# First feed-forward of a hybrid layer: table batches in finer steps, three sums in each, and four queues held to the text's order

## Chip, cores and metric

The kernel runs on one core of one Trainium2 chip. The metric is the device time of one execution in microseconds (us), the median of several runs. Engines are named as the profile names them: PE (TensorE, the matrix engine; PEld is its weight load), DVE (VectorE), ACT (ScalarE), POOL (GpSimd) and SP (SyncE, whose queue issues most DMAs here; "SPq" in the rows).

## The reference, cut to what matters

One decoder layer for 1024 tokens of width 1024, all in f32:

```python
mod = silu(cond) @ w_mod + b_mod              # nine vectors of 1024
h = modulate(rms_norm(x, ffn1_norm), sh1, sc1)
x = x + 0.5 * g1 * swiglu(h, w_gate, w_up, w_down)          # first feed-forward, d_ff = 2816
h = modulate(rms_norm(x, mix_norm), sh2, sc2)
b, c, v, u = split(h @ w_in)
y_conv = b * conv3_causal(c * v)
y_ssm  = GLU(Re(C . state) + D * u)           # 32 groups, 64 complex states each
x = x + g2 * ([rms_norm(y_conv) | rms_norm(y_ssm)] @ w_out)
x = x + 0.5 * g3 * swiglu(modulate(rms_norm(x, ffn2_norm), sh3, sc3), ...)   # second feed-forward
return rms_norm(x, final_norm)
```

Two kinds of side work do not depend on the tokens, and the kernel does them during the first feed-forward: the **modulation sums** (rows of `w_mod` times the activated condition, one row block of 128 x 1024 after another) and the **tables of the state space model** (powers of its eigenvalues times B and C), which the mixing stage reads later.

## The kernel before, in words

Every f32 product is three matrix products of rounded parts: each operand is a high part (fp32r) and a low part, and `mm3` issues high x high, high x low, low x high, 128 x 512 each. A weight tile `w` gets its parts in `Weights.pump`: ACT casts the raw tile to the high part, DVE subtracts to get the low part; the raw tile came by a DMA on SP, and some raw tiles get a second block added by a DMA on POOL.

The first feed-forward has 11 groups of 256 hidden channels, `fa0` to `fa10`. Groups 1 to 10 run in `seven`: gate and up projections as seven block products each (left operands A11, S1, S2, S4, S3, A12, A22, in that order for groups 2 to 10). One of the seven is 24 matrix products of 128 x 512, gate side then up side. They gather in three PSUM banks a side, called B, C and A; a bank is read out (ACT copies it to `t1`, `c1` or `u2`, or DVE adds it to one of these) before the next product in that bank may start. The products of a finished group go to DRAM (`kept1` to `kept10`). Then `down7`, twice (`fad0`, `fad1`), does the down projection of groups 1 to 8, again as seven products; it needs the kept blocks back as left operands: `fetch` loads one from DRAM on SP, ACT casts it, DVE subtracts (`fa1lA11` is block A11 of group 1). The fetches for `fad0` are issued inside `fa10`, four after each of its products. Groups 0, 9 and 10 follow in `last_parts` (tiles `fald`).

The side work is a Python generator, `side1`. A `Clock` counts the `mm3` calls; after every `period` ticks it runs the generator to its next `yield`, so the instructions of that step stand at that place in the program's text. The period is `BATCH_PERIOD` during the tables. The tables are made in eight batches, `ssm_batch(0)` to `ssm_batch(7)`. One batch: load `prm`; DVE makes `bb`, then `cl` (with a second term `clt`), `bl` (with `blt`) and the rotors `rot`, `rott`, from a pool of four buffers tagged `bt`; PE multiplies `bl` and `cl` into `kp` and transposes `bl` into `tp`, 8 short instructions; ACT copies these to `kc` and `mi` (again `bt` buffers); DVE corrects `kc`; SP stores all to DRAM: `mo_d` from `cl`, `co_d` and `si_d` from the rotors, `mk_d` from `kc`, `mi_d` from `mi`. `gate1` is one modulation sum: `mod_tile` lets DVE do the sum over the oldest loaded tile (`ISA wm...` in the program order) and SP load the next one; there are two such tiles.

Before group 10 starts, the text says (lines 1355 to 1361)

```python
if g == NGRP - 1:
    while clock.side:
        clock.step()
    side_open.close()
    ...
    open_x(ctx)
    load_x(range(2), (0, 2))
```

so whatever is left of the batches is written down at once between `fa9` and `fa10`; the memory of the tables is then given back, and four loads of `x` go into it.

The order in which an engine gets its instructions is not always the text's. A scheduler lays the program out ahead of time from its own idea of when things are ready, engine by engine, and may move an instruction past others of the same engine. `InOrder` wraps VectorE, ScalarE, TensorE and SyncE: while `InOrder.strict` is true, each instruction issued through it is tied behind the one before on that engine, so that this engine keeps the text's order. GpSimd is not wrapped. Before the change, strict order holds in the prologue alone. At run time every engine takes its instructions strictly one after the other.

Of the kernel before, what the change touches and what calls it, by code (L numbers as in the profile page):

```python
# [13 lines left out]
F32 = mybir.dt.float32  # L14
# [214 lines left out]
def hymba_layer(ctx: ExitStack, tc, x_d, xt_d, wm1_d, wmod_d, gu1_d, gs1_d, ds1_d, wl1_d, win_d, wout_d, glu_d, gu2_d, gs2_d, wd2_d, ds2_d, wl2_d, cols_d, cond_d, lam_d, bc_d, out_d):  # L229
# [771 lines left out]

    cact_d = scratch.tile([P, 1024], F32, name="cact_d")
    SP.dma_start(cact_d[:], cact[:])
    mk_d = scratch.tile([NB, P, GB * P], F32, name="mk_d")
    mi_d = scratch.tile([NB, P, GB * P], F32, name="mi_d")
    mo_d = scratch.tile([NB, P, GB * P], F32, name="mo_d")
    co_d = scratch.tile([NB, P, GB * P], F32, name="co_d")
# [25 lines left out]
    def ssm_base(sb, sb1):  # L1033
# [127 lines left out]
            yield  # L1161
        zero = sb1.tile([CH, 112], F32, name="zero")
        V.memset(zero[:], 0.0)
        mk4 = mk_d[:].rearrange("b p (g c) -> p b g c", g=GB)
        for t in range(1, TAU):
            for b in range(NB):
                SP.dma_start(
                    mk4[t * CH : (t + 1) * CH, b, :, 0 : t * CH],
                    zero[:, 0 : t * CH].unsqueeze(1).to_broadcast([CH, GB, t * CH]),
                )  # L1170
            yield
        ssm.update(q=qq, tabs=tabs, base=baset, step=step, lam=lam)

    def ssm_batch(b):
        bp = bps[0]
        gs = slice(b * GB, (b + 1) * GB)
        prm = bp.tile([P, 4, GB, CH], F32, tag="prm", name=f"prm{b}")
        SP.dma_start(prm[:], bc_d[b])
        bb = bp.tile([P, 2, GB, CH], F32, tag="bb", name=f"bb{b}")
        q = tuple(ssm["q"][:, i, gs].unsqueeze(2).to_broadcast([P, GB, CH]) for i in range(2))  # L1180
        cmul(bp, bb[:], prm[:, 0:2], q, [GB, CH], f"bb{b}")
        p1, p2, e1, e2 = ssm["tabs"]

        def bt(name):
# [12 lines left out]
        cl = bt(f"cl{b}")
        cl4 = cl[:].rearrange("p (g n c) -> p g n c", g=GB, n=9)
        yield from comb(cl4, 9, (p1, p2), (prm[:, 2], prm[:, 3]), ALU.add, f"clt{b}")
        SP.dma_start(mo_d[b].rearrange("p (g m) -> p g m", g=GB), cl4[:, :, 1:9, :].rearrange("p g n c -> p g (n c)"))  # L1200
        bl = bt(f"bl{b}")
        bl4 = bl[:, :512].rearrange("p (g n c) -> p g n c", g=GB, n=8)
        yield from comb(bl4, 8, (e1, e2), (bb[:, 0], bb[:, 1]), ALU.add, f"blt{b}")
        if b >= 2:
            yield from gate1()

        def v3(a):
            return a[:, :512].rearrange("p (g m i) -> p g m i", g=GB, m=8)

        bs = [a[:, gs, :].unsqueeze(2).to_broadcast([P, GB, 8, 16]) for a in ssm["base"]]  # L1210
        st = [ssm["step"][:, i, :, gs].rearrange("p m g -> p g m").unsqueeze(3).to_broadcast([P, GB, 8, 16]) for i in range(2)]

        def rotors():

            r, t = bt(f"rot{b}"), bt(f"rott{b}")
            V.tensor_tensor(out=v3(r), in0=st[0], in1=bs[0], op=ALU.mult)
            V.tensor_tensor(out=v3(t), in0=st[1], in1=bs[1], op=ALU.mult)
            yield
            V.tensor_tensor(out=r[:, :512], in0=r[:, :512], in1=t[:, :512], op=ALU.add)
            A.activation(t[64:128, :512], r[64:128, :512], AF.Copy, scale=-1.0)  # L1220
            for half in (slice(0, 64), slice(64, 128)):
                SP.dma_start(co_d[b, half], r[0:64, :512])
            SP.dma_start(si_d[b, 0:64], r[64:128, :512])
            SP.dma_start(si_d[b, 64:128], t[64:128, :512])

        yield from rotors()
# [10 lines left out]
        if b >= 2:  # L1237
            yield from gate1()
            yield from gate1()
            yield from gate1()  # L1240
        kc = bt(f"kc{b}")
        kc3 = kc[:CH, :512].rearrange("p (g m) -> p g m", g=GB)
        A.copy(kc[:CH, :512], kp[:])
        for g in range(GB):
            V.scalar_tensor_tensor(
                out=kc3[:, g, 0:CH], in0=ident[:CH, :CH], scalar=ssm["lam"][:CH, 3, b * GB + g : b * GB + g + 1], in1=kc3[:, g, 0:CH], op0=ALU.mult, op1=ALU.add
            )
        mk3 = mk_d[b].rearrange("p (g m) -> p g m", g=GB)
        for t in range(TAU):
            SP.dma_start(mk3[t * CH : (t + 1) * CH, :, t * CH :], kc3[:, :, : P - t * CH])  # L1250
        mi = bt(f"mi{b}")
        A.copy(mi[:, :512], tp[:])
# [39 lines left out]
    def side1():  # L1292
        yield from combos1()
        clock.period = 4.5
        sb = side_open.enter_context(tc.tile_pool(name="sb", bufs=1, side="right"))
        with tc.tile_pool(name="sb1", bufs=1, side="right") as sb1:
            yield from ssm_base(sb, sb1)
        clock.period = BATCH_PERIOD
        bps.append(side_open.enter_context(tc.tile_pool(name="bp", bufs=1, side="right")))
        mod_home.pool = side_open.enter_context(tc.tile_pool(name="wmp", bufs=1, side="right"))  # L1300
        share[0] = MODS[1]
        for _ in range(2):
            mod_fetch(mod_home)
        for b in range(NB):
            yield from ssm_batch(b)

    def side2(home, n):

# [16 lines left out]
            norm_into(act2, h, n2[h], 1, "h2")  # L1325

    movs["B"] = es1.enter_context(tc.tile_pool(name="movB1", bufs=12))
    BATCH_PERIOD = 5.5
    first_open = ExitStack()

    def first_opened():
# [32 lines left out]
        seven(f"fa{g}", kept=kept[g], order=SOON if g == 1 else SEVEN, then=(lambda left: fetch_chunk(0, left)) if g == NGRP - 1 else None)  # L1364
    down7("fad0", lefts[0], 0, lambda left: fetch_chunk(1, left), lambda left: load_x(range(2), (1, 3)) if left == "A12" else None)
    down7("fad1", lefts[1], 0, fetch_last)
    clock.period = 4
    clock.side.append(side2(mod_mov, MODS[2]))
    pools["mixed"] = False
# [454 lines left out]
```

## Time and profile before

| what | value |
|---|---|
| time, median of 3 runs | 1688.69 us (1688.16 to 1690.33) |
| profiled execution, its own time | 1691.52 us |
| its span, first to last instruction | 1689.7 us |
| instructions | 20647 |
| PE busy | 1657.2 us, 98% |
| DVE, ACT, POOL busy | 63%, 40%, 10% |

How to read the rows. A timeline row gives start, length, engine, line, operation, the tile written and those read, the shape and how many instructions were merged into the row; in brackets stands how long the engine sat idle before it, and what ended that. All instructions issued through the wrapper have line L111, so tiles tell them apart, and buffer numbers are left out (`kp` for `kp0` to `kp7`; `fa7gB` is group 7, gate side, bank B). A windows row gives, for a stretch of the span, the busy time of each engine with its number of instructions, the granted clock of PE as a share of full speed, the share of the DMA engines and GB/s. A wait row names who waited, for whom, the total, how often and the longest. A DMA row gives the issuing queue, the number and size of transfers and the median time from issue to landing. PE counts as busy from the start of a matrix product to a modelled end, so its waits are read from the gaps.

### The profile page before, as it was taken

How to read it: one execution, taken by the hardware profiler on the slowest of the kernel's cores; microseconds unless marked ns; L12 is line 12 of the kernel's file. 1: busy time of each engine (PE TensorE's matmuls, PEld its weight loads, DVE VectorE, ACT ScalarE, POOL GpSimd, SP SyncE). 2: the span in 40 equal slices, each digit the busy share in tenths (PEclk: the TensorE clock that was granted, in tenths of full speed). 3: DMA queues.
4: the chain of work that ended last, by engine and by line, in shares of the span. 5: the costliest groups of instructions: out<-in, count | busy, mean ns of one | idle time of the engine just before them, and what ended most of it. 6: DMA issues, size and time to landing. Idle time of an engine off the chain costs nothing.

```text
span 1689.7 us, 20647 instructions
## 1 busy us (share of the span) xinstructions
PE 1657.2 (98%) x7521; PEld 1364.8 (81%) x7521; DVE 1065.5 (63%) x1581; ACT 676.8 (40%) x992; POOL 169.4 (10%) x207
## 2 busy tenths in 40 slices
PE   8999989999999999999999999999999999999997
PEld 5888878878888888787878778888888888888887
DVE  7984787766567758735656848856555655444454
ACT  6654333333454431332214316434444444322234
POOL 2010000001001102100000121000001101010003
PEclk9999999999999999999999999999999999999999
DMA  9477987987898767145653324558887787989812
GB/s 352 136 165 180 263 253 210 271 235 202 258 315 232 183 210 281 39 112 163 199 158 110 103 97 150 133 140 220 239 227 206 218 222 218 321 271 341 263 55 100
DMA packets 129128, 340.21 MB, mean 201 GB/s; under 512 B 22401, under 2 KB 38017, under 8 KB 128002
## 3 DMA queue, kind: packets, MB, share of 16 engines
q1 hardware_dynamic: 112898, 280.16, 47.9%
q0 software_dynamic: 16128, 58.73, 20.1%
q8 instruction: 59, 0.97, 0.2%
q14 instruction: 43, 0.35, 0.1%
HBM read 254.41 MB, written 76.02 MB: 196 GB/s over the span
## 4 chain that ended last, share of the span: by engine, by line
PE 70%; DVE 7%; DMA 6%; issue 2%; SPq 1%; ACT 0%; POOL 0%; DVEq 0%; POOLq 0%; ACTq 0%
PE fald L111 4%; PE wo L111 3%; PE fad_0B L111 3%; PE fbd_0B L111 3%; PE fad_1B L111 3%; PE fbd_1B L111 3%; PE fb10d L111 2%; PE u L111 2%; PE b L111 2%; DMA wm<-in_wmod 2%; DMA swx<-X 2%; PE c L111 1%; DMA raw<-in_gs 1%; PE fad_0C L111 1%; PE fb0u L111 1%
## 5 line engine op out<-in xcount | busy, mean ns | idle before, releaser
L111 DVE TENSOR_TENSOR w<-raw,w 128x1024 fp32r<-128x1024 f32 x242 | 296.3, 1226 | 264.2 <-ACT w L111 263.9
L111 ACT CAST w<-raw 128x1024 fp32r<-128x1024 f32 x242 | 254.0, 1051 | 310.9 <-DMA raw<-in_ds 60.2
L173 POOL DMA_DIRECT2D raw<-in_gs x80 | 70.6, 885 | 741.9 <-DVE w L111 454.0
L111 DVE CUSTOM_DVE_ANT_0 wm<-wm,cact 128x1024 f32<-128x1024 f32 x56 | 76.0, 1370 | 36.3 <-DMA wm<-in_wmod 31.6
L173 POOL DMA_DIRECT2D raw<-in_ds x32 | 28.1, 877 | 281.4 <-DVE w L111 178.6
L111 PE MATMUL p<-h,w 128*128 128x512 f32 x192 | 49.4, 407 | 1.3 <-ACT h L111 1.0
L111 PE MATMUL wo<-oa,w 128*128 128x512 f32 x192 | 45.5, 391 | 2.9 <-ACT w L111 2.2
L111 PE MATMUL wo<-ob,w 128*128 128x512 f32 x192 | 45.6, 392 | 1.1 <-ACT ob L111 0.6
L111 PE MATMUL v<-h,w 128*128 128x512 f32 x192 | 46.0, 393 | 0.0
L111 PE MATMUL c<-h,w 128*128 128x512 f32 x192 | 46.0, 393 | 0.0
L111 PE MATMUL b<-h,w 128*128 128x512 f32 x192 | 45.1, 392 | 0.0
L111 PE MATMUL u<-h,w 128*128 128x512 f32 x192 | 44.8, 392 | 0.2 <-DVE h L111 0.2
L111 PEld LDWEIGHTS wo<-oa,w 128*128 128x128 f32 x192 | 35.8, 188 | 11.1 <-ACT w L111 2.6
L111 PEld LDWEIGHTS p<-h,w 128*128 128x128 f32 x192 | 35.7, 192 | 9.6 <-ACT h L111 1.6
L111 PEld LDWEIGHTS wo<-ob,w 128*128 128x128 f32 x192 | 35.7, 188 | 9.2 <-ACT ob L111 1.0
L111 PEld LDWEIGHTS u<-h,w 128*128 128x128 f32 x192 | 35.7, 188 | 8.3 <-DVE h L111 0.6
L111 PEld LDWEIGHTS b<-h,w 128*128 128x128 f32 x192 | 35.7, 188 | 7.2
L111 PEld LDWEIGHTS v<-h,w 128*128 128x128 f32 x192 | 35.5, 188 | 7.1
L111 PEld LDWEIGHTS c<-h,w 128*128 128x128 f32 x192 | 35.5, 188 | 7.0
L111 DVE SCALAR_TENSOR_TENSOR x<-fb10d,gate,x 128x512 f32<-128x512 f32 (+1 forms) x20 | 12.9, 643 | 24.4 <-PE fb10d L111 24.3
L111 DVE TENSOR_TENSOR X<-co,X 128x512 f32<-128x512 f32 x8 | 5.5, 692 | 35.3 <-DMA swx<-X 27.5
L111 PE MATMUL fb10d<-fb9lA,w 128*128 128x512 f32 (+1 forms) x120 | 25.6, 347 | 0.0
(1532 smaller groups left out, 3866.5 us busy)
## 6 DMA issues: line engine op xcount, KB each, us to landing
raw<-in_gs SPq DMA_DIRECT2D x80, 512.0 KB, 4.9
raw<-in_gs POOLq DMA_DIRECT2D x80, 512.0 KB, 6.6
wm<-in_wmod SPq DMA_DIRECT2D x56, 512.0 KB, 6.8
raw<-in_ds SPq DMA_DIRECT2D x32, 512.0 KB, 5.9
raw<-in_ds POOLq DMA_DIRECT2D x32, 512.0 KB, 7.3
mw<-in_wm SPq DMA_DIRECT2D x8, 1024.0 KB, 8.9
raw<-in_win SPq DMA_DIRECT2D x16, 512.0 KB, 4.3
raw<-in_wl SPq DMA_DIRECT2D x10, 512.0 KB, 4.3
```

What stands on the lines that cost most here:

```text
L111: r = getattr(self.engine, name)(*args, **kw)
L173: self.G.dma_start(out=r[:], in_=src, accum_op=ALU.add)
```

## The change

Three things change, all in the side work of the first feed-forward, and a switch.

1. **Finer steps.** `ssm_batch` yields after nearly each DVE operation: 13 steps where there were 5 (batches 0 and 1) or 9 (with four sums). `BATCH_PERIOD` goes from 5.5 to 2.9 ticks. Each batch now holds exactly three sums, after its 2nd, 6th and 10th step, where batches 0 and 1 had none and the others four, three of them in a row. `prm` of the next batch is loaded earlier, and the rotors' stores stand one step after the rotors, behind the short matrix products.
2. **`mk_d` laid out otherwise.** It becomes one flat piece of DRAM with rows twice as wide, so that the eight shifted copies of `kc` are one store with a constant stride: 4 stores of 16 x 8 x 128 per batch instead of 8 of falling width, and 7 stores of zeros instead of 56. `out_loads` reads it later in pieces of 512 bytes.
3. **Strict order** is switched on when the first batch begins and off after `fad1`. It spans groups 4 to 10 and both `down7`.

```diff
-        for t in range(1, TAU):
-            for b in range(NB):
-                SP.dma_start(
-                    mk4[t * CH : (t + 1) * CH, b, :, 0 : t * CH],
...
+        for t in range(1, TAU):
+            SP.dma_start(
+                mk4[t * CH : (t + 1) * CH, :, 0 : t * CH],
...
-        mk3 = mk_d[b].rearrange("p (g m) -> p g m", g=GB)
-        for t in range(TAU):
-            SP.dma_start(mk3[t * CH : (t + 1) * CH, :, t * CH :], kc3[:, :, : P - t * CH])
+        for g in range(GB):
+            SP.dma_start(mk_steps[b][:, :, g, :], kc3[:, g, :].unsqueeze(1).to_broadcast([CH, TAU, P]))
...
-        if b >= 2:
-            yield from gate1()
-            yield from gate1()
-            yield from gate1()
+        A.activation(t[64:128, :512], r[64:128, :512], AF.Copy, scale=-1.0)
+        for half in (slice(0, 64), slice(64, 128)):
+            SP.dma_start(co_d[b, half], r[0:64, :512])
+        SP.dma_start(si_d[b, 0:64], r[64:128, :512])
+        SP.dma_start(si_d[b, 64:128], t[64:128, :512])
+        yield
...
+        prm_load(0)
         for _ in range(2):
             mod_fetch(mod_home)
+        yield
+        InOrder.strict = True
         for b in range(NB):
-            yield from ssm_batch(b)
+            for i, _ in enumerate(ssm_batch(b)):
+                yield
+                if i % 4 == 1:
+                    yield from gate1()
...
-    BATCH_PERIOD = 5.5
+    BATCH_PERIOD = 2.9
...
     down7("fad1", lefts[1], 0, fetch_last)
+    InOrder.strict = False
```

What the switch and the new steps do to the queues is seen in the order of the built programs. On **PE, where group 9 ends and group 10 begins**, there stood before:

```order
L111 MATMUL fa9uB_3401<-h15_1_453,w66_3512 128x512 x3
L111 MATMUL fa9uB_3401<-h16_1_491,w66_3512 128x512 x3
L111 MATMUL fa9uB_3401<-h17_1_534,w66_3512 128x512 x3
L111 MATMUL kp7_3707<-cl7_3628,bl7_3663 16x128 x4
L111 MATMUL tp7_3712<-ident_84,bl7_3663 128x128 x4
L111 MATMUL fa10gB_3759<-h10_0_194,w67_3549 128x512 x3
```

There stands now:

```order
L111 MATMUL fa9uB_3284<-h17_1_534,w66_3408 128x512 x3
L111 MATMUL kp6_3574<-cl6_3419,bl6_3477 16x128 x4
L111 MATMUL tp6_3579<-ident_84,bl6_3477 128x128 x4
L111 MATMUL kp7_3631<-cl7_3609,bl7_3618 16x128 x4
L111 MATMUL tp7_3636<-ident_84,bl7_3618 128x128 x4
L111 MATMUL fa10gB_3678<-h10_0_194,w67_3449 128x512 x3
```

The matrix products of batch 6 moved here from the middle of group 9; those of batch 7 stay ahead of the first product of group 10. On **DVE**, the operations that make `bl7` stood in the middle of group 9 before, between the additions of its C bank:

```order
L111 TENSOR_TENSOR w66_3512<-raw37_3141,w66_3512 128x1024
L111 TENSOR_TENSOR fa9gu2_3483<-fa9gu2_3483,fa9gC_3425 128x512
L111 TENSOR_TENSOR bl7_3663<-tab2_1488,bb7_3621 128x512
L111 TENSOR_TENSOR blt7_3664<-tab3_1489,bb7_3621 128x512
L111 TENSOR_TENSOR bl7_3663<-bl7_3663,blt7_3664 128x512
L111 TENSOR_TENSOR fa9uu2_3510<-fa9uu2_3510,fa9uC_3444 128x512
```

Now the end of batch 6 and all of batch 7 follow the last read-out of group 9 (`fa9Y` from bank `fa9uB`), first

```order
L111 TENSOR_TENSOR fa9Y_3447<-fa9uB_3284,fa9c21_3550 128x512
L111 TENSOR_TENSOR w70_3567<-raw41_3357,w70_3567 128x1024
L111 ISA wm3_2_0_3434,mods_93<-wm3_2_0_3434,cact_100 128x1024
L111 ISA mods_93 128x1
L111 SCALAR_TENSOR_TENSOR kc6_3589<-ident_84,lam_907,kc6_3589 16x16 x4
L111 TENSOR_TENSOR bb70_3603<-prm7_3475,qq_1320 128x128
L111 TENSOR_TENSOR bb71_3604<-prm7_3475,qq_1320 128x128
L111 TENSOR_TENSOR bb7_3602<-bb70_3603,bb71_3604 128x64 x2
```

and right behind these

```order
L111 TENSOR_TENSOR cl7_3609<-tab0_1486,prm7_3475 128x576
L111 ISA wm3_2_1_3508,mods_93<-wm3_2_1_3508,cact_100 128x1024
L111 ISA mods_93 128x1
L111 TENSOR_TENSOR clt7_3610<-tab1_1487,prm7_3475 128x576
L111 TENSOR_TENSOR cl7_3609<-cl7_3609,clt7_3610 128x576
L111 TENSOR_TENSOR bl7_3618<-tab2_1488,bb7_3602 128x512
L111 TENSOR_TENSOR blt7_3619<-tab3_1489,bb7_3602 128x512
L111 ISA wm3_3_0_3572,mods_93<-wm3_3_0_3572,cact_100 128x1024
L111 ISA mods_93 128x1
L111 TENSOR_TENSOR bl7_3618<-bl7_3618,blt7_3619 128x512
```

so `bl7` moved from the middle of group 9 to behind its end, with three sums ahead of it. On **SP at the same place** the stores of batch 6's rotors, which stood among the stores of group 8 before, now stand behind the load of a sum's tile:

```order
L111 DMA kept9Y_658<-fa9Y_3447 128x1024
L111 DMA wm3_3_0_3572<-in_wmod 128x1024
L111 DMA co_d_693<-rot6_3537 64x512 x2
L111 DMA si_d_694<-rot6_3537 64x512
L111 DMA si_d_694<-rott6_3538 64x512
L111 DMA mk_d_690<-kc6_3589 16x8x128 x4
L111 DMA mi_d_691<-mi6_3591 128x512
```

That load goes into the buffer of `wm3_2_0`, so it is issued when that sum is done; `bb70` and `bb71` take the `bt` buffers of `rot6` and `rott6`. The third place is **ACT in group 10**. Before, the copies of bank C (`fa10gc1`, `fa10uc1`) stood ahead of the casts of the third and fourth fetched block:

```order
L111 CAST fa1lA11_3794<-fa1lA11_3794 128x512
L111 CAST fa2lA11_3798<-fa2lA11_3798 128x512
L111 COPY fa10gt1_3772<-fa10gB_3759 128x512
L111 COPY fa10ut1_3787<-fa10uB_3774 128x512
L111 CAST w71_3789<-raw42_3515 128x1024
L111 COPY fa10gc1_3823<-fa10gC_3810 128x512
L111 COPY fa10uc1_3838<-fa10uC_3825 128x512
L111 CAST w72_3840<-raw43_3653 128x1024
L111 CAST fa3lA11_3802<-fa3lA11_3802 128x512
```

Now they stand behind all four:

```order
L111 COPY fa10ut1_3706<-fa10uB_3693 128x512
L111 CAST w71_3708<-raw42_3411 128x1024
L111 CAST fa1lA11_3713<-fa1lA11_3713 128x512
L111 CAST fa2lA11_3717<-fa2lA11_3717 128x512
L111 CAST fa3lA11_3721<-fa3lA11_3721 128x512
L111 CAST fa4lA11_3725<-fa4lA11_3725 128x512
L111 COPY fa10gc1_3742<-fa10gC_3729 128x512
L111 COPY fa10uc1_3757<-fa10uC_3744 128x512
```

The two copies moved behind `fa3lA11` and `fa4lA11`; the first two casts moved behind the copies of bank B.

More of the change, by code (lines that the diff above doesn't have):

```diff
@@ L1003, in hymba_layer @@
     SP.dma_start(cact_d[:], cact[:])
-    mk_d = scratch.tile([NB, P, GB * P], F32, name="mk_d")
+    mk_row = NB * GB * 2 * P
+    mk_all = scratch.tile([P * mk_row + P], F32, name="mk_d")
+    mk_d = mk_all[: P * mk_row].rearrange("(p b g m) -> b p g m", p=P, b=NB, g=GB)[:, :, :, :P]
+    mk_steps = mk_all[:].rearrange("(t r) -> t r", t=TAU)[:, : CH * mk_row].rearrange("t (c b g m) -> b c t g m", c=CH, b=NB, g=GB)[:, :, :, :, :P]
     mi_d = scratch.tile([NB, P, GB * P], F32, name="mi_d")
@@ L1163, in ssm_base, with prm_load @@
         V.memset(zero[:], 0.0)
-        mk4 = mk_d[:].rearrange("b p (g c) -> p b g c", g=GB)
+        mk4 = mk_all[: P * mk_row].rearrange("(p q m) -> p q m", p=P, q=NB * GB)
         for t in range(1, TAU):
-            for b in range(NB):
-                SP.dma_start(
-                    mk4[t * CH : (t + 1) * CH, b, :, 0 : t * CH],
-                    zero[:, 0 : t * CH].unsqueeze(1).to_broadcast([CH, GB, t * CH]),
-                )
+            SP.dma_start(
+                mk4[t * CH : (t + 1) * CH, :, 0 : t * CH],
+                zero[:, 0 : t * CH].unsqueeze(1).to_broadcast([CH, NB * GB, t * CH]),
+            )
             yield
         ssm.update(q=qq, tabs=tabs, base=baset, step=step, lam=lam)
+    def prm_load(b):
+        ssm["prm"] = bps[0].tile([P, 4, GB, CH], F32, tag="prm", name=f"prm{b}")
+        SP.dma_start(ssm["prm"][:], bc_d[b])
     def ssm_batch(b):
@@ L1176, in ssm_batch @@
         gs = slice(b * GB, (b + 1) * GB)
-        prm = bp.tile([P, 4, GB, CH], F32, tag="prm", name=f"prm{b}")
-        SP.dma_start(prm[:], bc_d[b])
+        prm = ssm["prm"]
         bb = bp.tile([P, 2, GB, CH], F32, tag="bb", name=f"bb{b}")
@@ L1200, in ssm_batch @@
         SP.dma_start(mo_d[b].rearrange("p (g m) -> p g m", g=GB), cl4[:, :, 1:9, :].rearrange("p g n c -> p g (n c)"))
+        if b + 1 < NB:
+            prm_load(b + 1)
         bl = bt(f"bl{b}")
@@ L1211, in ssm_batch @@
         st = [ssm["step"][:, i, :, gs].rearrange("p m g -> p g m").unsqueeze(3).to_broadcast([P, GB, 8, 16]) for i in range(2)]
[L1213 to L1226, printed above, removed]
+        r, t = bt(f"rot{b}"), bt(f"rott{b}")
+        V.tensor_tensor(out=v3(r), in0=st[0], in1=bs[0], op=ALU.mult)
+        yield
+        V.tensor_tensor(out=v3(t), in0=st[1], in1=bs[1], op=ALU.mult)
+        yield
+        V.tensor_tensor(out=r[:, :512], in0=r[:, :512], in1=t[:, :512], op=ALU.add)
         yield
@@ L1236, in ssm_batch @@
             T.transpose(tp[:, g * P : (g + 1) * P], bl[:, g * P : (g + 1) * P], ident[:])
-        if b >= 2:
-            yield from gate1()
-            yield from gate1()
-            yield from gate1()
+        A.activation(t[64:128, :512], r[64:128, :512], AF.Copy, scale=-1.0)
[3 more added lines that the diff above has]
+        SP.dma_start(si_d[b, 64:128], t[64:128, :512])
+        yield
         kc = bt(f"kc{b}")
@@ L1243, in ssm_batch @@
         A.copy(kc[:CH, :512], kp[:])
+        mi = bt(f"mi{b}")
+        A.copy(mi[:, :512], tp[:])
+        yield
         for g in range(GB):
@@ L1247, in ssm_batch @@
             )
-        mk3 = mk_d[b].rearrange("p (g m) -> p g m", g=GB)
-        for t in range(TAU):
-            SP.dma_start(mk3[t * CH : (t + 1) * CH, :, t * CH :], kc3[:, :, : P - t * CH])
-        mi = bt(f"mi{b}")
-        A.copy(mi[:, :512], tp[:])
+        for g in range(GB):
+            SP.dma_start(mk_steps[b][:, :, g, :], kc3[:, g, :].unsqueeze(1).to_broadcast([CH, TAU, P]))
         SP.dma_start(mi_d[b], mi[:, :512])
@@ L1301, in side1 @@
         share[0] = MODS[1]
+        prm_load(0)
         for _ in range(2):
             mod_fetch(mod_home)
+        yield
+        InOrder.strict = True
         for b in range(NB):
-            yield from ssm_batch(b)
+            for i, _ in enumerate(ssm_batch(b)):
+                yield
+                if i % 4 == 1:
+                    yield from gate1()
     def side2(home, n):
```

## Prediction

> **What bounds the kernel now.** I read the page first, then the windows, then the waits of PE over the stretch that the change touches, then the timelines of PE and DVE at those waits and where group 9 ends. PE is the bound almost everywhere, so a microsecond that PE waits is a microsecond of the kernel. The page's first line and four windows (start and end; then PE, PEld, DVE, ACT, POOL busy with instructions, PE's clock, DMA share, GB/s):
>
> ```profile
> span 1689.7 us, 20647 instructions
> 200.00:300.00 100.00, 95.61 (x436) 77.61 (x435) 67.20 (x118) 32.84 (x47) 7.10 (x8) 1.00 0.82 240
> 300.00:400.00 100.00, 97.85 (x439) 79.38 (x438) 77.45 (x128) 36.72 (x52) 9.72 (x11) 0.98 0.90 243
> 480.00:660.00 180.00, 179.93 (x793) 148.36 (x792) 125.02 (x166) 75.18 (x110) 17.05 (x16) 1.00 0.80 237
> 700.00:1000.00 300.00, 288.61 (x1392) 239.38 (x1391) 177.41 (x274) 86.55 (x129) 18.80 (x13) 1.00 0.45 135
> ```
>
> PE lacks 4.4 us and 2.2 us in the two stretches in which the tables are made, and nothing during `fad0` and `fad1`. The mixing stage lacks 11.4 us, but the change leaves its order alone. All waits of PE from 60 to 480 us are three:
>
> ```profile
> PE kp L111 <- DVE bl L111: 3.3, 1, 3.3
> PE fa7gB L111 <- DVE fa7gc L111: 2.1, 1, 2.1
> PE fa5gC L111 <- DVE w L111: 1.1, 1, 1.1
> ```
>
> They sum to 6.5 us, each on a DVE that came late. The timeline of PE shows one more cost, at the wait of 2.1 us (start, length):
>
> ```profile
> 347.60 2.88 PE L111 MATMUL fa7uA<-h,w 128*128 128x512 f32 x12
> 352.55 4.57 PE L111 MATMUL fa7gB<-h,w 128*128 128x512 f32 x12 [2.06 <-DVE fa7gc L111]
> ```
>
> Behind it the same twelve products take 4.57 us where they take 2.88: 1.7 us more, PE's clock being lower for a while. The wait of 3.3 us had no such tail, as the clock of its window, 1.00, shows.
>
> **What the change can take away.** The three waits and the slow tail: 6.5 + 1.7 = 8.2 us, if DVE is never late again. In finer steps it should seldom be: between `bl`'s last addition and `kp` now stand four steps of 2.9 ticks, and one tick is three products, 0.68 us, so some 8 us, and a bank is read by DVE at least one product of 5.4 us before it is needed. I leave 0.5 us for small waits that the text's order makes in batches 0 to 6, with 4 us as the other end.
>
> **Costed at nothing.** The loads of `mk` in the mixing stage and PE's wait there (issue ns; landing; who waits):
>
> ```profile
> L111 SPq DMA_DIRECT2D mk<-mk_d x8: 325/326/581, 621.3 to 866.6; - x8
> DMA to landing us min/median/max: 2.9/3.9/6.6
> PE yy L111 <- DVE co L111: 4.9, 4, 2.8
> ```
>
> The stores of zeros and the four wider stores of `kc`: SP issues fewer DMAs, and PE has no wait on SP's work in these stretches; without that cover they could only give time back. The 512-byte pieces in which `mk` is loaded later: the loads land in 3.9 us, are issued a whole batch ahead of use (16 ticks, 11 us), and PE waits there for `co`, not for `mk`; were they to take three times as long, the cover would be gone and each of eight batches could lose a microsecond. POOL's queue is not held to the text and hardly changes. In `last_parts` the scheduler now puts a few products of the second token half ahead of some of the first; the work is the same.
>
> **What the change adds: the end of group 9.** PE, DVE and the DMAs there, before:
>
> ```profile
> 436.29 2.88 PE L111 MATMUL fa9uB<-h,w 128*128 128x512 f32 x12
> 439.10 1.05 PE L111 MATMUL kp<-cl,bl 128*16 128x128 f32 x8
> 440.49 2.98 PE L111 MATMUL fa10gB<-h,w 128*128 128x512 f32 x12
> 421.30 0.69 DVE L111 TENSOR_TENSOR bl<-tab,bb 128x512 f32<-128x512 f32 x1
> 421.90 0.69 DVE L111 TENSOR_TENSOR blt<-tab,bb 128x512 f32<-128x512 f32 x1
> 422.62 0.69 DVE L111 TENSOR_TENSOR bl<-bl,blt 128x512 f32<-128x512 f32 x1
> 439.28 0.69 DVE L111 TENSOR_TENSOR fa9Y<-fa9uB,fa9c 128x512 f32<-128x512 f32 x1 [2.89 <-PE fa9uB L111]
> 440.33 1.23 DVE L111 TENSOR_TENSOR w<-raw,w 128x1024 fp32r<-128x1024 f32 x1 [0.36 <-ACT w L111]
> ```
>
> Before, `bl7` is ready at 423.3, 16 us before `kp7` needs it, and PE goes from group 9 through `kp7` and `tp7` into group 10 without a gap. Now `bl7` stands on DVE behind `fa9Y`, which waits for the last product of group 9. Call that end T0 (439.2 above). PE takes 1.3 us more for `kp6` and `tp6`, then it stands at `kp7` until DVE has gone through the whole row shown in the section on the change. All of group 10 is queued behind `kp7`. The durations (groups of DVE from 200 to 480 us: busy time, mean ns):
>
> ```profile
> L111 DVE CUSTOM_DVE_ANT_0 wm<-wm,cact 128x1024 f32<-128x1024 f32 x19 | 23.2, 1221 | 17.9 <-DMA wm<-in_wmod 17.9
> L111 DVE TENSOR_TENSOR cl<-cl,clt 128x576 f32<-128x576 f32 x7 | 5.3, 752 | 0.0
> L111 DVE SCALAR_TENSOR_TENSOR kc<-ident,lam,kc 16x16 f32<-16x16 f32 x32 | 5.3, 217 | 2.0 <-ACT kc L111 2.0
> L111 DVE TENSOR_TENSOR bl<-bl,blt 128x512 f32<-128x512 f32 x7 | 4.8, 687 | 0.1
> L111 DVE TENSOR_TENSOR bb<-prm,qq 128x128 f32<-128x128 f32 x14 | 3.7, 281 | 5.8 <-PE kp L111 3.2 <-DMA si_d<-rot 2.6
> L111 DVE TENSOR_TENSOR bb<-bb,bb 128x64 f32<-128x64 f32 x14 | 2.6, 217 | 0.1
> ```
>
> The instructions alone: `fa9Y` 0.69, `w70` 1.23, three sums 3.66, four `kc` 0.87, `bb` 0.56 + 0.43, three of `cl` and `clt` at 0.75, three of `bl` and `blt` at 0.69: 11.8 us. Neighbours start 0.60 apart where one takes 0.69, so about 0.08 goes off each of some 15 joints, and `w70` waits 0.36 for its cast: 11.0 us. PE's wait is then at least 11.0 - 1.3 = 9.7 us.
>
> On top comes a wait through SP. `bb70` and `bb71` need the buffers of the rotors, whose stores stand behind the load of `wm3_3_0`, and this is issued only when the sum `wm3_2_0` is done: T0 + 1.1 + 1.1 + 1.2 = T0 + 3.5. The DMAs (median us to landing; for the stores also the time of one issue, ns):
>
> ```profile
> wm<-in_wmod SPq DMA_DIRECT2D x24, 512.0 KB, 6.5
> co_d<-rot SPq DMA_DIRECT2D x16, 128.0 KB, 4.3
> si_d<-rot SPq DMA_DIRECT2D x8, 128.0 KB, 5.4
> si_d<-rott SPq DMA_DIRECT2D x8, 128.0 KB, 5.1
> L111 SPq DMA_DIRECT2D co_d<-rot x16: 457/506/1454, 191.9 to 428.9; - x16
> L111 SPq DMA_DIRECT2D si_d<-rot x8: 448/684/1051, 195.2 to 429.6; - x8
> ```
>
> With 0.4 for the load, two issues of 0.51 and one of 0.68, the last store is issued at T0 + 5.6 and lands at T0 + 10.7. Then `bb71`, `bb7`, `cl7`, the second sum and the rest: 7.5 us less ten joints of 0.08, 6.7 us. `bl7` is ready at T0 + 17.4 and PE has waited **16.1 us**. The tile of the third sum is issued at T0 + 3.5 and lands at T0 + 10, ahead of need. The ends for this cost: 9.7 us if the stores land at once, 21 us if they land 2 or 3 us later than the median and DVE itself reaches `fa9Y` 2 us late (by its order it has three or four operations of 0.69, a `w` of 1.23 and part of a batch for each of the last products of group 9, about 6 us in 5.4).
>
> **The clock after it.** After the wait of 2.06 us the trace lost 1.7 us, after that of 3.3 us nothing. For 16 us of idleness I take **1.7 us**; ends 0 and 3.4. The Trainium skill, "TensorE: Matmul & The Clock Gate", section "Part 1: The HAM clock gate", has the clock halve after an idle window of about 3.4 us and recover after a busy one of that length. The length of the tail in the trace agrees; that 2.06 us of idleness were enough does not, and there the measurement decides. By the page the removed waits, all under 3.4 us, would give back 6.5 us and not 8.2, and the sum would be 1.7 us higher.
>
> **Inside group 10.** Here ACT keeps the text's order: the four casts of the blocks A11, which wait for DMAs, now stand ahead of the copies of bank C (`fa10gc1`), and the fourth product (S4, into bank C again) needs those copies. What came when before (SP, then ACT, then landing):
>
> ```profile
> 442.15 6.24 SPq L111 DMA_DIRECT2D mk_d<-kc  x8
> 450.10 1.86 SPq L111 DMA_DIRECT2D x<-in_x  x4
> 452.00 0.56 SPq L111 DMA_DIRECT2D fa4lA<-kept4X  x1
> 448.95 0.59 ACT L111 COPY fa10gc<-fa10gC 128x512 f32<-128x512 f32 x1 [1.19 <-PE fa10gC L111]
> 461.09 0.60 ACT L111 CAST fa4lA<-fa4lA 128x512 fp32r<-128x512 f32 x1
> 456.91 2.88 PE L111 MATMUL fa10gC<-h1S,w 128*128 128x512 f32 x12
> fa4lA<-kept4X SPq DMA_DIRECT2D x1, 256.0 KB, 8.3
> ```
>
> The last block landed 452.0 + 8.3 - 442.1 = 18 us after `kc7` was done (SP's first store of it), for the loads of `x` must wait until all table stores have landed. Now `kc7` is done 3.8 us after `bl7` (three rotor operations at 0.6, a sum 1.2, 0.8 for the rest), so the block lands about 21.8 us after `kp7` starts, cast and copy end at 23.0. Fewer stores are issued ahead of it (some 2 us saved) but all four fetches stand behind `x`, so I keep the 18. The fourth product would start 456.9 - 440.5 = 16.4 after group 10 begins, that is at 1.4 + 1.7 + 16.4 = 19.4. PE waits **3.6 us** more; ends 0 and 8. A slow clock behind that wait has the two cases of the trace for and against it: half of 1.7, **0.9 us**. `fad0` itself had its blocks 17 us early (`fa4lA` cast at 461.1, needed when `fad0` starts, seven products of 5.44 after 440.5), which covers the shift; in the second half of `fad0` the same order stands on ACT (casts of a block ahead of the next copies) with a microsecond to spare: **0.5 us**, up to 3.
>
> **The sum.** -8.2 + 0.5 + 16.1 + 1.7 + 3.6 + 0.9 + 0.5 = +15.1 us. The profiled execution took 1691.5 us, 1.8 over its span and 2.8 over the median of the runs; the terms are differences, so I add them to the median, 1688.7: **1704 us**, 0.9% slower.
>
> **The rivals.** *Bare burst, not slower by more than 0.2%*: the stores of batch 6 land before DVE asks, the burst runs at its 11.0 us, and ACT's copies of bank C are not held up. Then 9.7 + 1.7 - 8.2 = +3.2 us: 1692 us, and 1690 if the clock holds. For it: the landing times above are medians, and none of these rows excludes a quicker one. Against: they are not even issued before T0 + 4. It decides at 11.5 us of wait: below that the change is within 0.2%. *Burst without the second wait*: the fetched blocks land 4 us sooner, since SP has less to issue; 1699 us. *The text's order costs in every batch*: each batch's `bb` waits for the stores of the one before, which are issued 6 us ahead and land in 5, and the evacuations of PSUM queue behind it. 1.2 us in each of seven batches: 1712 us. For it: `bb` waited 2.6 us for `si_d` once already. Against: a bank has 5.4 us to spare. *Something outside gets faster*: the mixing stage would have to lose its 11.4 us of waits and the removed 8.2 besides; I see no cause.
>
> **How the numbers follow.** Forecast 0.55, second wait absent 0.20, costs in every batch 0.13, bare burst 0.09, gain elsewhere 0.03. The range takes in the first three with their ends and most of the bare burst's upper side: 1694 to 1713 us. A difference of 0.2%, 3.4 us, is about what a measurement of this kernel can tell from none. Two thirds of the bare burst lie within it: same 0.06; faster 0.03; slower 0.91.
>
> **What would show it.** In the profile after: a wait `kp <- DVE bl` of 14 to 18 us near 440, with `bb<-prm` waiting some 6 us for `si_d` inside it; a stretch at half clock after it; a wait of `fa10gC` on ACT of a few us some 16 us later; no waits of `fa5gC` or `fa7gB`. I am wrong if `kp` waits under 11 us, or if several waits of PE appear between 200 and 430.

## The result, and the profile after

The changed kernel takes 1761.9 us (median of 4 runs, 1761.4 to 1762.4) where the one before takes 1688.5 (1688.2 to 1690.3): a ratio of 1.043, 95% interval 1.042 to 1.044. It is slower, as forecast, but by 73 us and not by 15. The page's first line and its first section:

```profile
span 1760.6 us, 20541 instructions
PE 1675.0 (95%) x7521; PEld 1375.2 (78%) x7521; DVE 1070.3 (61%) x1581; ACT 678.9 (39%) x992; POOL 169.8 (10%) x207
```

PE is busy for 1675.0 us, 18 more than before for the same 7521 instructions, so part of the loss is slow clock and the rest waiting. The windows say where (us; then PE, PEld, DVE, ACT, POOL busy with instructions, PE's clock, DMA share, GB/s):

```profile
200.00:300.00 100.00, 100.00 (x456) 81.77 (x454) 73.36 (x119) 35.96 (x49) 8.82 (x10) 1.00 0.83 229
300.00:400.00 100.00, 100.00 (x458) 81.92 (x458) 76.59 (x125) 37.95 (x53) 8.84 (x10) 1.00 0.90 256
400.00:450.00 50.00, 33.05 (x153) 26.66 (x153) 34.97 (x63) 14.09 (x20) 3.53 (x4) 0.85 0.73 210
450.00:500.00 50.00, 36.51 (x144) 28.89 (x143) 18.37 (x29) 17.70 (x29) 1.77 (x2) 0.91 0.68 212
500.00:550.00 50.00, 40.63 (x155) 32.86 (x156) 26.73 (x35) 19.65 (x29) 3.53 (x4) 0.83 0.60 155
550.00:600.00 50.00, 44.27 (x182) 35.43 (x180) 19.85 (x26) 17.39 (x26) 2.64 (x3) 0.93 0.72 214
600.00:650.00 50.00, 41.26 (x163) 33.55 (x164) 35.50 (x48) 18.93 (x29) 5.28 (x6) 0.90 0.57 144
```

While the tables are made PE is now full; the 4.4 and 2.2 us that it lacked before are gone. From 400 to 650 it lacks 54 us, and the clock is low besides; before, `fad0` and `fad1` had no gap. And from 450 to 600 us DVE is busy for 65 of 150 us (18.37 + 26.73 + 19.85), ACT for 55, the DMAs for two thirds: something is late, not something full. The longest waits of PE in the first feed-forward (us in total, times, longest):

```profile
PE kp L111 <- DVE bl L111: 17.0, 1, 17.0
PE fad_0B L111 <- ACT fad_0t L111: 11.9, 2, 9.1
PE fa10gB L111 <- DVE fa10gc L111: 6.1, 1, 6.1
PE fad_0B L111 <- DVE fad_0c L111: 5.9, 1, 5.9
PE fad_0B L111 <- ACT fad_0u L111: 5.2, 1, 5.2
PE fa10gB L111 <- ACT fa10gu L111: 5.0, 1, 5.0
PE fald L111 <- DVE x L111: 3.5, 3, 2.0
PE fald L111 <- ACT fa10lA L111: 3.1, 1, 3.1
PE fa10gC L111 <- ACT fa10gc L111: 2.7, 1, 2.7
```

The first is the wait forecast, the last the one forecast at 3.6 us. The seven between were not. Taken by the start of PE's products, stage by stage (us; a stage runs from its first product to that of the next; negative leads are ahead):

| stage | before | after | difference |
|---|---|---|---|
| lead at the last product of group 9 (`fa9uB` 436.29, 425.61) | | | -10.7 |
| from there to the first product of group 10 | 4.2 | 24.0 | +19.8 |
| group 10 | 38.2 | 59.1 | +20.9 |
| `fad0` and `fad1` | 152.9 | 187.8 | +34.9 |
| last parts (`fald`) | 67.1 | 76.7 | +9.6 |
| everything behind | | | -3.5 |

Together 71 us, the difference of the spans. The second row is the forecast's burst; the three rows behind it, 65 us, were to cost 5.

**The loop.** The chain of work that ended last, taken over the stretch from 440 to 520 us, spells the cause out (start, length, who; the pieces called "issue" and SP's issues between 483.30 and 484.68 are left out):

```profile
473.91 4.91 DMA fa3lS<-kept3Z
478.84 0.62 ACT fa3lS L111
479.48 0.62 ACT fa4lS L111
480.10 0.49 ACT fa10gu L111
480.59 0.49 ACT fa10uu L111
481.07 0.95 ACT w L111
482.05 1.24 DVE w L111
483.30 0.33 SPq L111
484.68 7.02 DMA fa3lS<-kept3W
491.72 0.62 ACT fa3lS L111
```

Read it as a circle: a fetched block lands; ACT casts it, and only then the bank copies and the next weight; DVE subtracts that weight and so frees its raw buffer; this lets SP go on, whose next instruction in the text is the raw load into that buffer (483.30) with the next four fetches behind it; these must land before ACT can go on. Every link stands in its queue where the text put it. SP's raw loads and two rows of PE show the period, in the timeline:

```profile
459.28 0.33 SPq L111 DMA_DIRECT2D raw<-in_ds  x1
472.54 0.33 SPq L111 DMA_DIRECT2D raw<-in_ds  x1
483.30 0.33 SPq L111 DMA_DIRECT2D raw<-in_ds  x1
480.64 5.42 PE L111 MATMUL fa10gB<-h1S,w 128*128 128x512 f32 x12 [5.02 <-ACT fa10gu L111]
500.29 5.46 PE L111 MATMUL fa10gB<-h,w 128*128 128x512 f32 x12 [6.07 <-DVE fa10gc L111]
```

One lap is 483.30 - 472.54 = 10.8 us; one product of group 10, which uses up one weight and has four fetches written behind it, is 5.44. PE therefore falls behind by some 5 us a lap, and the two waits shown, of 5.02 and 6.07, are each followed by twelve products that take 5.4 us and not 2.88. Four products of seven have such a raw load ahead of their fetches: behind 483.30 the next one goes out at 508.90, and in the second half of `fad0` three go out at 566.85, 578.02 and 588.98, laps of 11.2 and 11.0 us. In the kernel before, the same raw loads at this place went out at the pace of the products (the third at 459.93):

```profile
449.05 0.34 SPq L111 DMA_DIRECT2D raw<-in_ds  x1
454.49 0.33 SPq L111 DMA_DIRECT2D raw<-in_ds  x1
```

SP can close the circle with another instruction than a raw load. The longest wait in these stages, 9.1 us in `fad0`, ends when the last of the four fetches behind this store has landed and been cast. The store waits for `fa10Y`, and this stands on DVE behind the subtractions of the four blocks fetched before:

```profile
516.99 0.68 DVE L111 TENSOR_TENSOR fa10Y<-fa10uB,fa10c 128x512 f32<-128x512 f32 x1
517.70 0.32 SPq L111 DMA_DIRECT2D kept10Y<-fa10Y  x1
```

### The profile page after: what moved, and what is told of

It is laid out like the page before. It is cut to its first block, busy times and chain, and to the rows that moved or that the text cites. A ratio compares the mean times of both kernels' runs of the same rounds, so it can differ in the third digit from the quotient of the medians.

```text
span 1760.6 us, 20541 instructions
## 1 busy us (share of the span) xinstructions
PE 1675.0 (95%) x7521; PEld 1375.2 (78%) x7521; DVE 1070.3 (61%) x1581; ACT 678.9 (39%) x992; POOL 169.8 (10%) x207
## 3 DMA queue, kind: packets, MB, share of 16 engines
q1 hardware_dynamic: 115058, 281.07, 46.2%
## 4 chain that ended last, share of the span: by engine, by line
PE 76%; DVE 9%; DMA 9%; issue 2%; ACT 2%; SPq 1%; POOL 0%; DVEq 0%; POOLq 0%; ACTq 0%
PE wo L111 3%; PE fbd_1B L111 2%; PE fbd_0B L111 2%; PE p L111 2%; PE fb10d L111 2%; PE fad_0B L111 2%; DMA swx<-X 2%; PE u L111 2%; PE fad_1B L111 2%; DVE w L111 2%; DMA wm<-in_wmod 1%; PE b L111 1%; DVE wm L111 1%; PE fb0u L111 1%; PE fb0g L111 1%
## 5 line engine op out<-in xcount | busy, mean ns | idle before, releaser
L111 PEld LDWEIGHTS p<-h,w 128*128 128x128 f32 x192 | 35.1, 189 | 10.6 <-ACT h L111 2.0
L111 PE MATMUL fald<-fa0lA,w 128*128 128x512 f32 x96 | 25.1, 413 | 3.5 <-DVE x L111 3.5
L111 PEld LDWEIGHTS fald<-fa0lA,w 128*128 128x128 f32 x96 | 18.9, 200 | 8.9 <-DVE x L111 4.8
```

The costliest lines, as they stand in the source:

```text
L111: r = getattr(self.engine, name)(*args, **kw)
```

## The experiments

The theory is this LOOP. Its rivals: BURST, the 17 us wait makes the fetches late and all else follows from it; COPIES, the prediction's own, only ACT's copies behind the casts cost; others are named where they come. The table has for each kernel how far ahead (-) or behind it begins group 10 against the kernel before, the stages in us, and the 95% interval of the ratio of its time to that of the kernel before on the same chip (1687.5 to 1689.1 us there).

| kernel | at group 10 | group 10 | `fad0`, `fad1` | last parts | time | ratio |
|---|---|---|---|---|---|---|
| before | 0 | 38.2 | 152.9 | 67.1 | 1688.5 | |
| after | +9.1 | 59.1 | 187.8 | 76.7 | 1761.9 | 1.042 to 1.044 |
| order off at group 10 | -10.6 | 40.0 | 161.8 | 67.1 | 1691.0 | 1.000 to 1.002 |
| order off behind the burst | -10.9 | 46.8 | 155.9 | 67.1 | 1690.8 | 1.000 to 1.002 |
| order from group 10 only | +14.2 | 61.2 | 190.8 | 79.9 | 1774.6 | 1.050 to 1.053 |
| period 2.35 | -9.6 | 59.5 | 189.3 | 77.9 | 1751.3 | 1.036 to 1.039 |
| ACT free | +8.2 | 62.3 | 182.0 | 78.8 | 1761.3 | 1.042 to 1.045 |
| DVE free | +8.8 | 50.2 | 187.8 | 79.6 | 1754.7 | 1.037 to 1.040 |
| ACT and DVE free | +8.5 | 38.5 | 153.7 | 69.1 | 1701.9 | 1.006 to 1.009 |
| SP free | +11.8 | 46.2 | 159.7 | 67.1 | 1714.2 | 1.014 to 1.018 |
| casts written later | +8.8 | 39.3 | 155.2 | 78.0 | 1713.7 | 1.014 to 1.017 |
| no order at all | +3.1 | 39.8 | 160.2 | 67.1 | 1703.1 | 1.007 to 1.010 |
| 2.35, order off at group 10 | -8.9 | 38.1 | 158.6 | 67.1 | 1686.8 | 0.999 to 1.001 |
| 2.35, ACT and DVE free | -9.2 | 38.1 | 162.1 | 69.4 | 1690.0 | 0.999 to 1.002 |
| 2.35, late casts, off ahead of `fad1` | -9.1 | 38.6 | 155.5 | 67.1 | 1685.6 | 0.996 to 0.999 |

**Where the order holds.** The four first runs move the two ends of the strict order, or the burst. Order off at group 10:

```diff
             while clock.side:
+                InOrder.strict = False
                 clock.step()
...
-    InOrder.strict = False
```

> The strict order ends just before what is left of the batches is written down ahead of group 10; everything else of the change stays. By stages the changed kernel stood 10.7 us ahead of the one before when group 9 ended, lost 19.8 at the tables' rest, 20.9 in group 10, 27.3 in fad0, 7.5 in fad1 and 9.6 in the parts behind it, and won 3.5 at the end. Theory LOOP (from group 10 on the text's order on four queues makes a round trip that takes longer than the product it feeds): all of the losses go, the 10.7 stay, some of the rest of the tables may still be waited for: 1678 to 1686 us. Rival BURST (the 17 us wait for bl7 and all that it makes late): the same, as the rest of the tables is free too. Rival FINER STEPS (the steps and the layout of mk_d cost by themselves, strict or not): 1740 us or more.

Of the 65 us 1.8 are left in group 10 and 8.9 in `fad0` and `fad1`; the rest goes. But these eat up just the lead of 10.6 us, so the time is 1691.0 and not 1678 to 1686. PE loses most of it at the start of `fad0`, waiting for one fetched block:

```profile
482.97 0.79 PE L111 MATMUL fad_0C<-fa4lS,w 128*128 128x512 f32 x1 [5.43 <-ACT fa4lS L111]
...
485.34 1.48 PE L111 MATMUL fad_1C<-fa1lS,w 128*128 128x512 f32 x3
```

with slow clock behind it (three products take 1.48 us, elsewhere 0.84). Order off behind the burst (the same line, one statement later, so that the rest of the tables stays in the text's order):

> The strict order ends behind the rest of the tables, just before the first product of group 10: on DVE, ACT and SP that rest stands in the text's order at the end of group 9 as in the changed kernel, the fetches come as late as there, but from there on the four queues are free. LOOP: the losses from group 10 on go (65 us less the 3.5 won at the end), and PE can go past the products of batch 7: 1680 to 1697 us. BURST: the fetched blocks are late as before, and group 10, fad0 and fad1 stay slow; only the wait of 17 us can be covered: 1735 to 1755 us. Rival COPIES (the prediction's: only ACT's copies of the PSUM banks behind the casts): as LOOP, 1680 to 1697.

1690.8, as LOOP and COPIES had it; 8.6 us are left in group 10 (4.3 of them the wait for `bl7`, since PE goes past `kp7` first) and 3.0 in `fad0` and `fad1`. It speaks less against BURST than I had meant it to: SP, being free, brought three of the first four fetches forward, to 426 to 431 us, so here they were not as late as in the changed kernel. The next two runs do better. The reverse, the batches without order and the order from group 10 on:

```diff
-        InOrder.strict = True
...
             while clock.side:
                 clock.step()
+            InOrder.strict = True
```

> The reverse: the batches and their rest are free, the strict order holds only from the first product of group 10 to the end of fad1. LOOP: group 10, fad0, fad1 and what follows lose about what they lose in the changed kernel, 20.9 + 27.3 + 7.5 + 9.6 - 3.5 = 62 us, on 1680 to 1690: 1735 to 1755 us. BURST: with the tables made in time the order behind them costs a few us: 1685 to 1700 us. COPIES: the fourth product of group 10 waits 4 us: 1685 to 1695 us.

The three stages lose 73.7 us ((61.2 + 190.8 + 79.9) - 258.2), as LOOP has it and more; the time passes its range by 20 us, since the rest loses besides: group 9 ends 4.9 us late (the batches without order, below), and 9.3 more are lost from there to group 10, where PE waits 6.5 us for `bl7`. And one number, `BATCH_PERIOD = 2.35`:

> One number: the batches' period 2.35 ticks where it is 2.9, the strict order as in the changed kernel. The tables are then all written down inside group 9, and nothing is left to be done at once ahead of group 10. LOOP: only the 19.8 us of the rest go, the later losses stay: 1738 to 1746 us. BURST: nothing is late any more: 1680 to 1690 us. COPIES: 1684 to 1694 us.

Here group 10 begins 9.6 us ahead and with nothing left to be done at once; the stages behind lose 68.5 us all the same. BURST falls: the burst and the loop are two costs that don't need each other.

**Which queue closes the loop.** The order is kept, and one engine after the other is let out of it from the first product of group 10 on:

```diff
-            if self.last is not None and InOrder.strict:
+            if self.last is not None and InOrder.strict and self.tied:
...
             while clock.side:
                 clock.step()
+            A.tied = False
```

> The changed kernel with ACT alone free from the first product of group 10 on; PE, DVE and SP keep the text's order. The rest of the tables (19.8 us) stays as it is. LOOP (SP's raw load, then the fetches, their landing, ACT's casts, the cast of the weight behind them, DVE's subtraction, SP's next raw load): cut on ACT, since the weight's cast and the copies no longer stand behind the casts of blocks that wait for their landing; of the 62 us lost behind the rest of the tables more than two thirds come back: 1698 to 1720 us. COPIES (only the copies of the PSUM banks stand behind the casts): the same range, so this run alone does not part them. Rival SP QUEUE (what hurts is SP alone: raw loads and fetches in the text's order make each fetch late): 1745 us or more.

No change in the time: 1761.3. This speaks against COPIES, whose whole mechanism is gone here: PE goes through six products of group 10 without a wait. My expectation for LOOP was wrong too, and the time lies in the range of SP QUEUE, by which SP's order alone makes the fetches late. PE now waits once, 21.1 us ahead of the seventh product, and the timeline of this kernel shows why:

```profile
474.76 1.22 DVE L112 TENSOR_TENSOR w<-raw,w 128x1024 fp32r<-128x1024 f32 x1
481.33 0.69 DVE L112 TENSOR_TENSOR fa1lS<-fa1lS 128x512 fp32r<-128x512 f32 x1 [5.35 <-ACT fa1lS L112]
...
484.80 0.69 DVE L112 TENSOR_TENSOR fa4lS<-fa4lS 128x512 fp32r<-128x512 f32 x1
485.41 1.22 DVE L112 TENSOR_TENSOR w<-raw,w 128x1024 fp32r<-128x1024 f32 x1
476.05 0.33 SPq L112 DMA_DIRECT2D raw<-in_ds  x1
486.70 0.33 SPq L112 DMA_DIRECT2D raw<-in_ds  x1
503.28 5.18 PE L112 MATMUL fa10gB<-h,w 128*128 128x512 f32 x12 [21.09 <-DVE fa10gc L112]
```

The subtractions of the fetched blocks stand ahead of the weight's on DVE as the casts do on ACT, so the same lap, 486.70 - 476.05 = 10.7 us, now runs over DVE. So the theory was put more sharply, as TWO LINKS, and DVE let out alone, then both (`V.tied = False`; `A.tied = V.tied = False`):

> The changed kernel with DVE alone free from the first product of group 10 on; PE, ACT and SP keep the text's order. With ACT alone free the time had stayed where it was, 1761 us, the subtractions of the fetched blocks standing ahead of the weight's on DVE. TWO LINKS (the loop closes over ACT's order or over DVE's, each alone is enough): the casts on ACT still hold up the weight's cast, 1740 to 1765 us. DVE LINK (the loop runs over DVE's order alone): 1698 to 1720 us.

> ACT and DVE both free from the first product of group 10 on; PE and SP keep the text's order, the rest of the tables as in the changed kernel. TWO LINKS: with both gone the loop is open though SP still has each raw load ahead of the fetches: 1698 to 1722 us, as with SP alone free (1714). SP QUEUE (SP's order alone makes the fetches late): 1740 us or more.

1754.7 and 1701.9. Either queue alone keeps the loop; with both out it is open, though SP still has every raw load ahead of the fetches, so SP QUEUE (1740 us or more) falls. SP now issues these loads at the pace of the products (463.30 - 457.99 = 5.3 us, then 5.4), and PE goes through group 10 without a wait:

```profile
457.99 0.37 SPq L112 DMA_DIRECT2D raw<-in_ds  x1
463.30 0.33 SPq L112 DMA_DIRECT2D raw<-in_ds  x1
468.74 0.33 SPq L112 DMA_DIRECT2D raw<-in_ds  x1
446.43 1.86 PE L112 MATMUL kp<-cl,bl 128*16 128x128 f32 x8 [16.97 <-DVE bl L112]
471.16 2.88 PE L112 MATMUL fa10gB<-h1S,w 128*128 128x512 f32 x12
```

The wait of 17.0 at `kp7` is untouched, and the first fetch goes out at 458.40 where it went at 459.65 in the changed kernel: as late, and it costs nothing more. Up to the last parts, which still lose 2.0 us, this kernel has the burst alone. At 1701.9 it is close to the prediction's sum without its waits inside group 10 and behind (1704 less 5.0). SP let out alone (`SP.tied = False`):

> The changed kernel with SP alone free from the first product of group 10 on; PE, DVE and ACT keep the text's order. LOOP: the round trip is cut on SP, fetches go out ahead of the raw load that waits for DVE, the casts on ACT find their blocks there: most of the 62 us come back, 1698 to 1720 us. COPIES: on ACT everything stands as before: 1750 to 1762 us. SP QUEUE: as LOOP, 1698 to 1720.

1714.2: the loop can be cut on SP as well, where fetches go ahead of the raw load that waits. Some of it stays (8.0 in group 10, 6.8 behind). Last, all queues kept in the text's order to the end, and the text changed: the cast and the subtraction of a fetched block are written two products behind its load.

```diff
-        A.copy(hi, whole_)
-        V.tensor_tensor(out=lo, in0=whole_, in1=hi.bitcast(F32), op=ALU.subtract)
+        def cast():
+            A.copy(hi, whole_)
+            V.tensor_tensor(out=lo, in0=whole_, in1=hi.bitcast(F32), op=ALU.subtract)
+        if late:
+            clock.after(late, cast)
+        else:
+            cast()
```

(`late` is 16 for `fad0` and `fad1`, nothing elsewhere.)

> The changed kernel, all four queues in the text's order to the end of fad1, but the cast (ACT) and the subtraction (DVE) of a fetched block of fad0 and fad1 are written 16 ticks, two products, behind its load. LOOP: each piece keeps its place but the casts, so a cast finds its block landed and nothing queues behind it; the loop is open and most of the 62 us come back: 1695 to 1715 us, with the 17 us wait at kp7 unchanged. COPIES: the same. SP QUEUE: SP's order is as in the changed kernel, so 1745 us or more. Rival HELD ORDER (holding four engines to the text costs by itself, whatever the text): 1740 us or more.

1713.7, with 39.3 us for group 10 and 155.2 for `fad0` and `fad1`: the order as such is not what costs (HELD ORDER falls), nor SP's place of the loads, but a wait for a landing that stands ahead of what the next load needs. The last parts, whose casts were left where they were, still lose 10.9 us.

**What the rest of the change is worth.** No order anywhere:

```diff
-        InOrder.strict = True
...
-    InOrder.strict = False
```

> The changed kernel without the strict order anywhere in this stretch: finer steps, three sums in each batch, the new layout of mk_d, and the scheduler's own order. LOOP: without the order no loop, and no rest of the tables held to the text: within 0.3% of the kernel before, 1684 to 1693 us; the table stage shows what the steps bring without the order, 0 to 10 us ahead when group 9 ends. Rival FINER STEPS (steps and layout cost by themselves): 1700 us or more.

1703.1, a miss: I had said 1684 to 1693, with 0 to 10 us of lead. It is 3.1 us behind at group 10, and 11.3 of loss are made in group 4 alone (`fa5gB` begins at 241.19, before at 229.86). Two rows of its waits in that stretch, 195 to 242 us:

```profile
DVE wm L111 <- DMA wm<-in_wmod: 14.6, 8, 4.0
PE fa4gB L111 <- DVE fa4gc L111: 4.9, 1, 4.9
```

The scheduler moves the sums forward, and DVE stands in front of PE's read-outs waiting for their tiles. FINER STEPS is right in that: without the order the steps cost. Most of it is made good by group 10, though; 1.6 us are lost in group 10 and 7.3 in `fad0` and `fad1`, where PE waits 1.8 us for ACT and 3.5 for DVE, and what makes these late was not traced. With the order, the same steps run without a gap of PE; the gain of the table stage belongs to the two together. Then the versions that should keep it. Period 2.35 with the order off at group 10:

> Period 2.35 and the strict order off where group 10 begins: the tables end inside group 9, four queues are free behind it. With the order off at group 10 and the period as in the changed kernel the time was that of the kernel before, 1691 against 1689: 10.6 us ahead at group 10, and these given back at the start of fad0, where the cast of a weight waits for its raw load ahead of the cast of the fetched block fa4lS. LOOP: no loop, as there; with batch 7 done and the memory of the tables free 17 us sooner, the four loads of x and the fetches behind them go sooner, the block is not late, and the gain stays: 1678 to 1684 us. Rival GIVEN BACK (the DMAs at the start of fad0 have a pace of their own, and whatever is won ahead is waited for there): 1686 to 1692 us.

Period 2.35 with ACT and DVE free:

> Period 2.35, and ACT and DVE free from the first product of group 10 on; PE and SP keep the text's order to the end of fad1. It asks whether the two costs add and nothing else is in the change: ACT and DVE free alone took 1701.9 us with the wait of 17.0 us at kp7 left in, period 2.35 alone 1751.3 with no such wait. ADD: 1701.9 less the 17.0 and about 2 us of slow clock and later start behind it, so 1681 to 1685 us, 9 us ahead at group 10 and about 6 still at the end of fad1. Rival GIVEN BACK (at the start of fad0 the DMAs take the lead away, as they did with the order off at group 10): 1686 to 1692 us. Rival THIRD COST (the text's order on SP and PE costs something yet unseen): above 1692 us.

And the three edits, period 2.35, late casts, and the order off ahead of `fad1`:

> Three edits of the changed kernel together: period 2.35, so that nothing of the tables is left at group 10; the casts and subtractions of fetched blocks written 16 ticks behind their loads; the strict order off ahead of fad1 and not behind it, since with it on the loads of the last parts stood in line on SP and the stage behind fad1 took 77.9 us where it takes 67.1. From stages: 9 us ahead when group 10 begins, about 1 lost in group 10, 1 in fad0, none later: 1679 to 1684 us. Rival GIVEN BACK (whatever is won ahead of fad0 is waited for there): 1686 to 1692 us.

The first, 1686.8, lies within 0.2% of the kernel before and at the edge of GIVEN BACK, above LOOP's 1678 to 1684; the second, 1690.0, is GIVEN BACK outright, and ADD is missed; the third is faster than both kernels, 1685.6, a ratio of 0.998 (0.996 to 0.999), some 3 us and not the 5 to 10 expected, between its two ranges. No third cost of the order shows ahead of the last parts, which lose 2.2 us in the second kernel. Of some 9 us of lead at group 10 there are left, where the last parts begin, 3.4, 0.2 and 6.1 us. The third alone has late casts, but it differs in more than that, so that they keep the lead is argued and not shown. Why it is lost is only partly seen: in the second kernel PE waits for DVE three times in the two down projections, 4.7 us together, and loses most of the other 4.4 of its 9.1 to the slow clock behind these waits; which transfer starts them was not traced.

## Why the prediction was wrong, point by point

- **The removed waits, -8.2 + 0.5**: right. All three are gone, and the lead at group 9's end is 10.7 us, of which 1.4 is `kp6` and `tp6` moved behind it; 9.3 against 7.7.
- **The end of group 9, +16.1**: right, with its mechanism. The wait is 17.0; inside it DVE waits for the rotors' stores, which were to land 10.7 us after `fa9Y` and did so after 439.50 - 428.60 = 10.9:

```profile
428.60 0.69 DVE L111 TENSOR_TENSOR fa9Y<-fa9uB,fa9c 128x512 f32<-128x512 f32 x1 [0.91 <-PE fa9uB L111]
439.50 0.49 DVE L111 TENSOR_TENSOR bb<-prm,qq 128x128 f32<-128x128 f32 x2 [6.91 <-DMA si_d<-rot]
447.01 1.86 PE L111 MATMUL kp<-cl,bl 128*16 128x128 f32 x8 [16.95 <-DVE bl L111]
449.57 4.00 PE L111 MATMUL fa10gB<-h,w 128*128 128x512 f32 x12
469.87 3.03 PE L111 MATMUL fa10gC<-h1S,w 128*128 128x512 f32 x12 [2.70 <-ACT fa10gc L111]
```

- **The clock after it, +1.7**: right. `kp7` takes 1.86 where it took 1.05, `tp7` 1.11 for 0.66 and the first product 4.00 for 2.98: 2.3 us. Up to the end of the first product of group 10 the forecast was +10.1 us, and the trace has the same, 9.1 at its start and 1.0 in it. That it fits so closely is luck: the gain is 1.6 us larger than forecast, the wait 0.9 longer and the slow clock 0.6 dearer.
- **Inside group 10, +3.6 + 0.9**: the one wait named there is in the trace, 2.70 us, 20 us after group 10 began; the slow clock behind it, put at 0.9, is hardly there (3.03 us where 2.88 is full clock). The step that failed is the one behind it: "which covers the shift" and "a microsecond to spare: 0.5 us". I took the fetches as a block that comes late once, by as much as the burst delays it, and counted 17 us of lead as proof against it. I read the order on ACT and followed none of what then waits: SP's raw load waits for DVE, DVE for ACT, ACT for the landing of fetches that SP has behind its last raw load. Such a circle has no lead to use up; it runs at 10.8 to 11.2 us a lap where PE needs 5.44. With the wait of 2.70 and the slow clock at its start, group 10 lost 20.9 us; `fad0` and `fad1` lost 34.9 and the last parts 9.6, where 5.0 had been forecast for all.
- **Costed at nothing, `mk_d`**: right. The waits of `yy` on `co` in the mixing stage are 3.6 us where they were 4.9, and PE waits for no `mk`.
- **The rivals**: none had the loop. The bare burst is out by the 17.0 us, and the burst without a second wait by the 2.70. "The text's order costs in every batch" was wrong in its place: between 200 and 400 us PE is full. What I had listed as signs came true one by one (the wait of 14 to 18 us, `si_d` inside it, the wait of `fa10gC` on ACT, no waits in the batches), and the time was still 58 us off. They all lay ahead of the fourth product of group 10; none would have shown a cost in the 227 us from there to the end of `fad1` (469.87 to 696.46), through which the order also held.

## What to carry to other kernels

Where queues are held to the text's order, don't look for the one instruction that moved behind a late one: follow the circle. Start at a load that waits for a buffer, go to the engine that frees it, to what stands ahead of that on its queue, to the transfer that this waits for, and to where its issue stands; if you come back to the load, one lap's length against the consumer's pace is the price, paid on each lap for as long as the order holds. It can be cut in the text, without giving up the order: issue the load, and write what waits for its landing one or two products later, on every engine that has such a part.

## What the runs showed of the hardware

- How long PE stood still does not say alone whether the clock drops. Behind 2.70 us twelve products took 3.03 us (2.88 at full clock), behind 5.02 and 6.07 they took 5.4; but behind 2.06 us in the kernel before they took 4.57, and with SP free they took 4.61 behind 2.23 us and 2.97 behind 2.93. The Trainium skill, "TensorE: Matmul & The Clock Gate", section "Part 1: The HAM clock gate", with its idle window of about 3.4 us, agrees with the waits of 2.70, 2.93, 5.02 and 6.07 us and not with those of 2.06 and 2.23.
- A burst alone costs little more than its wait: with ACT and DVE free, 17.0 us of wait became 19.8 between the last product of group 9 and the first of group 10, 1.4 of them products that were moved there, and nothing more in group 10 (38.5 us against 38.2).
- Of four 256 KB fetches issued together one was 4.9 us under way in one lap (the chain's row at 473.91) and 7.0 in the next (484.68): in the first of these laps, of 10.8 us, that is nearly half, though the DMAs are busy for only two thirds of the time.
